# The gate weights' low parts made by ScalarE and an accumulating DMA in place of a VectorE subtraction, in a two-layer streaming encoder

## The chip, the core and the metric

The kernel runs on one core of a Trainium2 chip. Its engines are TensorE (PE, whose weight loads the profile lists as PEld), VectorE (DVE), ScalarE (ACT), GpSimd (POOL) and SyncE (SP), which here does nothing but start DMAs; the core has 16 DMA engines. The metric is the device time of one execution in microseconds (us), lower is better. Three runs of the kernel before took 2331.43, 2334.34 and 2335.2 us; their median is 2334.34 us. The profile comes from one more execution, which took 2331.33 us, with a span of 2329.6 us from the first to the last instruction.

## What is computed

Two layers of an encoder work on 1056 tokens of width 1024 (1024 prompt tokens and 32 sample tokens). Each layer is a mixer, a SwiGLU feed-forward block, and at its end a gated embedding. All of it is in float32. Cut to what this change is about:

```python
def trunk(x, ple, ...):
    for i in range(2):
        ...                                   # mixer: pooling and convolution, or gating MLP and Mamba-2
        x = layer_norm(ALPHA * x + mix, ...)
        x = layer_norm(ALPHA * x + swiglu(x, w_ff1[i], w_ff3[i], w_ff2[i]), ...)
        x = x + (ple[i] @ w_ple[i]) * sigmoid(x @ w_ple_gate[i])
```

The change concerns `w_ple_gate`, 1024 x 1024 values per layer.

## The kernel before

**Products in three parts.** TensorE reads its operands in a rounded 32-bit form (F32R). To come near full float32 accuracy the kernel writes each operand as a high part (the rounded value) and a low part (the value less its high part), and makes each product from three matmuls: high weight by high input, low weight by high input, high weight by low input.

**The weights' supply.** The class `Weights` makes the weights in the order in which they are used. For a unit of 128 x 1024 values, `raw` (L76) starts a 512 KB load on SP's queue into one of two buffers `raw`. `split` (L86) then makes both parts in a tile `w` from a ring of four: ACT copies `raw` into the high part (L88), and DVE subtracts the high part from `raw` (L89). A buffer `raw` is free for the next load but one when both have read it. `get` (L136) hands out a unit and calls `prefetch`, which emits the making of further units until two whole units (four halves) are ready beyond the one in use. The instructions of each engine stand in one order, which a scheduler fixes when the program is built; each engine takes them strictly in that order, and a DMA's wait for its buffer is made by the engine that issues it.

**The gate stage.** `embed` (L1292) first makes the eight embedding products (L1310), which ACT copies to SBUF (L1315). Then come the gate products (L1331): for each half of the tokens, t = 0 and 1, for each of eight blocks m of 128 output features, 48 matmuls of 264 columns. So each of the eight gate units is made twice a layer: 16 units a layer, 32 in all. Behind each product ACT takes the sigmoid (L1337), DVE multiplies it with the embedding (L1338) and adds it to the residual stream (L1340), and behind every second one SP stores two rows of the stream (L1343). The PSUM tiles of these products, named `q`, are four in number.

**What lies around it.** The layer norm of the first token half, made by `norm` (L1402), is finished while the embedding products run, that of the second half during the gate products of the first half. Its small chain goes PE (statistics, L1412), DVE (L1425 to L1429), POOL (L1430, L1431, L1441) and back to PE (L1456). Then come the pieces: DVE multiplies and subtracts (L1479, L1480), ACT scales (L1482), and ACT and DVE split the result into `xhgate` and `xlgate` (L323, L324), which the gate products of that half read. In layer 0 the result of each half is split once more for layer 1, by the same two lines.

Of the kernel before, what the change touches and what calls it, by code (L numbers as in the profile page):

```python
# [9 lines left out]
AF = mybir.ActivationFunctionType  # L10
ALU = mybir.AluOpType
# [41 lines left out]
class Weights:  # L53
# [43 lines left out]
    def _make(self, order):  # L97
        for kind, key, src in order:
            if kind == "steps":
                yield from src()  # L100
            elif kind == "unit":
                raw = self.raw(src)
                yield key, 2, self.split(self.place()[:, :, :src.shape[1]], raw)
            elif kind == "22":
                yield key, 1, self.split(self.half(), self.raw(src[1][:, 512:1024]))
            else:

                r0, r1 = (self.raw(v) for v in src)
                a11, a12, a21, a22 = (r[:, h * 512:(h + 1) * 512] for r in (r0, r1) for h in range(2))
                own = lambda x: (key, 1, self.split(self.half(), x))  # L110
                if kind != "sums":
                    yield own(a11)
                    yield own(a12)
                s1 = self.sub(a21, a22, ALU.add)
                s2 = self.sub(s1, a11)
                if kind == "own":
                    yield own(self.sub(a12, s2))
                    continue
                yield own(s2)
                if kind == "all":  # L120
                    yield own(s1)
                yield own(self.sub(a11, a21))
                if kind == "sums":
                    yield own(s1)
                    continue
                yield own(self.sub(a12, s2))
                yield own(a22)
# [1480 lines left out]
```

## Time and profile before

| what | value |
|---|---|
| three runs, median | 2334.34 us (2331.43 to 2335.2) |
| the profiled execution | 2331.33 us |
| its span, first to last instruction | 2329.6 us |
| TensorE busy with matmuls | 2307.0 us, 99% of the span |
| VectorE busy | 1543.4 us, 66% |
| ScalarE busy | 966.1 us, 41% |
| GpSimd busy | 71.4 us, 3% |
| mean granted TensorE clock | 0.998 |
| moved by DMA | 207.37 MB, 89 GB/s over the span |

How to read it: a busy share is the part of the span in which an engine executed instructions; the shares overlap. The groups of instructions are listed by line of the kernel, engine, operation and tiles (written <- read), with their count, the busy time in all, the mean time of one in ns, and the idle time of the engine just before them with what ended it. "SPq" rows are DMA issues on SP's queue.

The gate products begin at 1009.1 us in layer 0 and end near 1107 us; in layer 1 they end the kernel, near 2323 us.

### The profile page before, as it was taken

How to read it: one execution, taken by the hardware profiler on the slowest of the kernel's cores; microseconds unless marked ns; L12 is line 12 of the kernel's file. 1: busy time of each engine (PE TensorE's matmuls, PEld its weight loads, DVE VectorE, ACT ScalarE, POOL GpSimd, SP SyncE). 2: the span in 40 equal slices, each digit the busy share in tenths (PEclk: the TensorE clock that was granted, in tenths of full speed). 3: DMA queues.
4: the chain of work that ended last, by engine and by line, in shares of the span. 5: the costliest groups of instructions: out<-in, count | busy, mean ns of one | idle time of the engine just before them, and what ended most of it. 6: DMA issues, size and time to landing. Idle time of an engine off the chain costs nothing.

```text
span 2329.6 us, 41097 instructions
## 1 busy us (share of the span) xinstructions
PE 2307.0 (99%) x17567; PEld 2273.9 (98%) x17567; DVE 1543.4 (66%) x2426; ACT 966.1 (41%) x1616; POOL 71.4 (3%) x88
## 2 busy tenths in 40 slices
PE   9999999999999999999999999999999999999998
PEld 8999999999999999999999989999999999999998
DVE  8755787544554978775556774787554454978773
ACT  5432354333333444474543562353333333434462
POOL 0000000000000000100000120100000000000100
PEclk9999999999999999999999999999999999999999
DMA  4113123222224621124212222022222225521132
GB/s 148 47 55 127 39 68 107 74 83 74 92 73 151 239 88 44 46 83 141 80 38 66 100 85 61 19 89 94 84 73 89 73 69 205 215 69 42 37 102 91
DMA packets 84378, 207.37 MB, mean 89 GB/s; under 512 B 10236, under 2 KB 19652, under 8 KB 84196
## 3 DMA queue, kind: packets, MB, share of 16 engines
q1 hardware_dynamic: 83428, 204.07, 26.5%
q8 instruction: 137, 2.24, 0.4%
q10 hardware_dynamic: 768, 0.68, 0.1%
q14 instruction: 45, 0.37, 0.1%
HBM read 171.57 MB, written 33.16 MB: 88 GB/s over the span
## 4 chain that ended last, share of the span: by engine, by line
PE 94%; DVE 3%; DMA 1%; POOL 1%; ACT 1%; issue 0%; SPq 0%; POOLq 0%; ACTq 0%
PE q L990 38%; PE q L1203 20%; PE q L1331 8%; PE mm L228 6%; PE mm L229 6%; PE mm L230 6%; PE q L1310 2%; PE mm L639 1%; PE mm L640 1%; PE mm L641 1%; DVE bf L94 1%; PE ms L775 1%; DVE w L89 1%; DMA raw<-w_out 1%; DMA raw<-w 0%
## 5 line engine op out<-in xcount | busy, mean ns | idle before, releaser
L1203 PE MATMUL q<-w 128*128 128x264 f32 x3696 | 457.0, 285 | 0.0
L1203 PEld LDWEIGHTS q<-w 128*128 128x128 f32 x3696 | 456.1, 188 | 0.0
L88 ACT ACTIVATE w<-raw 128x512 fp32r<-128x512 f32 (+2 forms) x246 | 185.7, 774 | 221.1 <-issue 76.3
L990 PE MATMUL q<-xhin,w 128*128 128x264 f32 x1664 | 270.7, 284 | 2.0 <-ACT xhin L963 0.8
L89 DVE TENSOR_TENSOR w<-raw,w 128x512 fp32r<-128x512 f32 (+2 forms) x246 | 212.8, 878 | 55.1 <-ACT w L88 54.8
L89 DVE TENSOR_TENSOR w<-bf,w 128x512 fp32r<-128x512 f32 (+1 forms) x250 | 167.0, 691 | 106.7 <-ACT w L88 105.5
L990 PEld LDWEIGHTS q<-xhin,w 128*128 128x128 f32 x1664 | 230.1, 188 | 3.0 <-ACT xhin L963 1.0
L88 ACT ACTIVATE w<-bf 128x512 fp32r<-128x512 f32 (+1 forms) x250 | 149.0, 629 | 195.9 <-PE q L990 77.9
L990 PE MATMUL q<-xhgate,w 128*128 128x264 f32 x1280 | 207.9, 284 | 0.6 <-DVE c L886 0.6
L228 PE MATMUL mm<-xhgate,w 128*128 128x384 f32 (+1 forms) x576 | 187.5, 326 | 1.1 <-ACT xhgate L323 1.1
L230 PE MATMUL mm<-xlgate,w 128*128 128x384 f32 (+1 forms) x576 | 186.1, 324 | 0.0
L229 PE MATMUL mm<-xhgate,w 128*128 128x384 f32 (+1 forms) x576 | 185.9, 323 | 0.0
L990 PEld LDWEIGHTS q<-xhgate,w 128*128 128x128 f32 x1280 | 176.8, 188 | 1.0 <-issue 0.8
L990 PE MATMUL q<-xlin,w 128*128 128x264 f32 x832 | 169.9, 285 | 0.6 <-DVE xlin L964 0.6
L1331 PE MATMUL q<-xhgate,w 128*128 128x264 f32 x1024 | 166.7, 285 | 0.0
L1331 PEld LDWEIGHTS q<-xhgate,w 128*128 128x128 f32 x1024 | 141.6, 188 | 0.0
L990 PE MATMUL q<-xlgate,w 128*128 128x264 f32 x640 | 130.0, 285 | 0.4 <-DVE xlgate L964 0.4
L990 PEld LDWEIGHTS q<-xlin,w 128*128 128x128 f32 x832 | 128.8, 188 | 1.3 <-DVE xlin L964 1.0
L228 PE MATMUL mm<-xhin,w 128*128 128x384 f32 (+1 forms) x384 | 125.5, 328 | 3.0 <-ACT w L88 1.8
L229 PE MATMUL mm<-xhin,w 128*128 128x384 f32 (+1 forms) x384 | 124.2, 325 | 0.6 <-DVE w L89 0.6
L94 DVE TENSOR_TENSOR bf<-raw 128x512 f32<-128x512 f32 x50 | 34.5, 691 | 135.8 <-DMA raw<-w 129.8
L230 PE MATMUL mm<-xlin,w 128*128 128x384 f32 (+1 forms) x384 | 123.9, 325 | 0.0
(329 smaller groups left out, 4305.7 us busy)
## 6 DMA issues: line engine op xcount, KB each, us to landing
raw<-w SPq DMA_DIRECT2D x116, 512.0 KB, 3.6
hidden<-c SPq DMA_DIRECT2D x44, 528.0 KB, 3.0
raw<-w_gate SPq DMA_DIRECT2D x32, 512.0 KB, 3.6
raw<-w_in SPq DMA_DIRECT2D x16, 512.0 KB, 3.8
raw<-w_out SPq DMA_DIRECT2D x16, 512.0 KB, 3.6
xhdown<-hidden SPq DMA_DIRECT2D x12, 528.0 KB, 7.7
t2down<-hidden SPq DMA_DIRECT2D x8, 528.0 KB, 3.8
t3down<-hidden SPq DMA_DIRECT2D x8, 528.0 KB, 3.9
```

Source lines behind the costliest of these rows:

```text
L88: self.nc.scalar.activation(hi, x, AF.Copy)
L89: self.nc.vector.tensor_tensor(lo, x, hi.bitcast(F32), op=ALU.subtract)
L94: self.nc.vector.tensor_tensor(t, a, b, op=op)
L228: nc.tensor.matmul(ps, wh, xh, start=first, stop=False)
L229: nc.tensor.matmul(ps, wl, xh, start=False, stop=False)
L230: nc.tensor.matmul(ps, wh, xl, start=False, stop=last)
L639: nc.tensor.matmul(o, xh, hi[:, s], start=k == 0, stop=False)
L640: nc.tensor.matmul(o, xh, lo[:, s], start=False, stop=False)
L990: nc.tensor.matmul(ps[:, a, :TH // 2], w[q][:, ks], x[r][:, k, a * TH // 2:(a + 1) * TH // 2], start=not add and k == 0 and j == 0, stop=k ...
L1203: nc.tensor.matmul(ps[m][:, a, :TH // 2], v[q][:, ms], x[r][:, a * TH // 2:(a + 1) * TH // 2], start=j == 0 and n == 0, stop=j == NG - 1 a ...
L1310: nc.tensor.matmul(ps[:, b, :TH // 2], w[q][:, o:o + P], pe[k][r][:, t * TH + b * TH // 2:t * TH + (b + 1) * TH // 2], start=k == 0 and i ...
L1331: nc.tensor.matmul(ps[:, b, :TH // 2], w[q][:, ks], token_half((self.xh, self.xl), k, t, b)[r], start=k == 0 and i == 0, stop=k == KD - 1 ...
```

## The change

For units whose key begins with `w_gate`, the low part is no longer a subtraction on DVE. ACT writes the high part as before, and then, with a second instruction on the same input and a scale of -1, writes the negated high part into the place of the low part. POOL then starts a DMA that reads `raw` from SBUF and adds it to what stands there, so that the place holds the raw value less its high part. All other weights are split as before.

```diff
             elif kind == "unit":
                 raw = self.raw(src)
-                yield key, 2, self.split(self.place()[:, :, :src.shape[1]], raw)
+                t = self.place()[:, :, :src.shape[1]]
+                if key[0].startswith("w_gate"):
+                    nc = self.nc
+                    nc.scalar.activation(t[:, 0, :], raw, AF.Copy)
+                    nc.scalar.activation(t[:, 1, :], raw, AF.Copy, scale=-1.0)
+                    nc.gpsimd.dma_start(out=t[:, 1, :], in_=raw, accum_op=ALU.add)
+                    yield key, 2, (t[:, 0, :], t[:, 1, :])
+                    continue
+                yield key, 2, self.split(t, raw)
```

DVE loses 32 instructions, ACT gains 32, and POOL's queue gains 32 DMAs. TensorE's order does not change. Lines from the old L104 on stand 8 lines lower in the changed kernel: the high part is L106 there, the negated part L107, the accumulating DMA L108, and the sigmoid L1345 (L1337 before).

Two places show the new order. The first is ACT in the second token half of layer 0's gate products; `w` is a gate unit, `bf` the sigmoid's result, `q` the product in PSUM. Before:

```order
L1337 ACTIVATE bf_11044<-q_10995 128x528
L88 ACTIVATE w_11109<-raw_11107 128x1024
L1337 ACTIVATE bf_11102<-q_11053 128x528
L88 ACTIVATE w_11167<-raw_11165 128x1024
L1337 ACTIVATE bf_11161<-q_11112 128x528
```

The same stretch now:

```order
L1345 ACTIVATE bf_11055<-q_11006 128x528
L106 ACTIVATE w_11121<-raw_11119 128x1024
L107 ACTIVATE w_11121<-raw_11119 128x1024
L1345 ACTIVATE bf_11114<-q_11065 128x528
L106 ACTIVATE w_11180<-raw_11178 128x1024
L107 ACTIVATE w_11180<-raw_11178 128x1024
L1345 ACTIVATE bf_11174<-q_11125 128x528
```

Each sigmoid now has two instructions on a weight unit ahead of it where it had one.

The second place is POOL's queue in the same stage of layer 0. The rows named `rn`, `t1down` and `t2down` belong to the layer norm, `cst` holds its identity matrix. Before, the norm of the first token half is followed directly by that of the second:

```order
L1441 TENSOR_TENSOR t2down_7482<-cst,rn_0_10133 128x384
L1441 TENSOR_TENSOR t2down_7482<-cst,rn_0_10133 128x256
L1430 TENSOR_TENSOR rn_1_10579<-sm_1_10578,mhalf 128x5
L1431 TENSOR_TENSOR rn_1_10579<-sm_1_10578,rn_1_10579 128x5
L1441 TENSOR_TENSOR t1down_7550<-cst,rn_1_10579 128x384
```

And now:

```order
L1449 TENSOR_TENSOR t2down_7482<-cst,rn_0_10133 128x384
L1449 TENSOR_TENSOR t2down_7482<-cst,rn_0_10133 128x256
L108 DMA w_10165<-raw_10163 128x1024
L108 DMA w_10307<-raw_10305 128x1024
L108 DMA w_10459<-raw_10457 128x1024
L108 DMA w_10524<-raw_10522 128x1024
L1438 TENSOR_TENSOR rn_1_10583<-sm_1_10582,mhalf 128x5
```

Four of the DMAs stand between the two norms on POOL; the other twelve of the layer follow behind the second norm.

## Prediction

> **What bounds the kernel now.** I read the page's head first, then who waits for whom on TensorE, then the groups and the timeline of the gate stage. The first two lines of the page:
>
> ```profile
> span 2329.6 us, 41097 instructions
> PE 2307.0 (99%) x17567; PEld 2273.9 (98%) x17567; DVE 1543.4 (66%) x2426; ACT 966.1 (41%) x1616; POOL 71.4 (3%) x88
> ```
>
> TensorE is idle for 22.6 us in all. No other engine can give more than that back, whatever is taken from it. TensorE's waits (line, what was waited for: us in total, times, longest):
>
> ```profile
> PE ms L1456 <- POOL dg L1441: 2.7, 4, 1.0
> PE q L1456 <- POOL t1down L1441: 2.0, 2, 1.0
> PE mm L228 <- ACT w L88: 1.8, 1, 1.8
> ...
> PE q L1456 <- POOL t2down L1441: 1.3, 2, 0.6
> ```
>
> Most are the norm's, waiting for POOL; none is at L1331, the gate products. The groups say the same (busy us, mean ns | idle before):
>
> ```profile
> L1331 PE MATMUL q<-xhgate,w 128*128 128x264 f32 x1024 | 166.7, 285 | 0.0
> ```
>
> So the subtractions that leave DVE are off the path now. In layer 0's gate stage, 1009 to 1110 us, they and their neighbours by shape are:
>
> ```profile
> L89 DVE TENSOR_TENSOR w<-raw,w 128x1024 fp32r<-128x1024 f32 x18 | 21.9, 1219 | 0.8 <-ACT w L88 0.7
> L88 ACT ACTIVATE w<-raw 128x1024 fp32r<-128x1024 f32 x18 | 18.9, 1051 | 0.5 <-DMA raw<-w_gate 0.5
> L323 ACT ACTIVATE xhgate<-stream 128x1056 fp32r<-128x1056 f32 x13 | 14.1, 1082 | 2.5 <-PE q L1331 0.9 <-DVE pre L523 0.7 <-DVE stream L1340 0.7
> ```
>
> What matters instead is how a unit gets to TensorE in time. The second token half shows the rhythm undisturbed; ACT first, then DVE, then SP's queue:
>
> ```profile
> 1066.51 0.61 ACT L1337 ACTIVATE bf<-q 128x528 f32<-128x528 f32 x1 [2.49 <-PE q L1331]
> 1067.01 1.05 ACT L88 ACTIVATE w<-raw 128x1024 fp32r<-128x1024 f32 x1
> 1072.33 0.61 ACT L1337 ACTIVATE bf<-q 128x528 f32<-128x528 f32 x1 [4.27 <-PE q L1331]
> 1072.84 1.05 ACT L88 ACTIVATE w<-raw 128x1024 fp32r<-128x1024 f32 x1
> 1078.16 0.61 ACT L1337 ACTIVATE bf<-q 128x528 f32<-128x528 f32 x1 [4.27 <-PE q L1331]
> ...
> 1068.52 1.22 DVE L89 TENSOR_TENSOR w<-raw,w 128x1024 fp32r<-128x1024 f32 x1
> ...
> 1064.05 6.04 SPq L79 DMA_DIRECT2D raw<-w_gate  x2
> ...
> 1075.59 0.33 SPq L79 DMA_DIRECT2D raw<-w_gate  x1
> ```
>
> A sigmoid comes as soon as its product ends, so two products take 1078.16 - 1066.51 = 11.65 us. The high part begins 0.50 us behind a sigmoid. It is made for the product after next, so it and the low part have about 11.1 us. The second load of the pair goes out at about 1069.8 us (1064.05 + 6.04 - 0.33), just when the subtraction ends (1068.52 + 1.22 = 1069.74): with two buffers `raw`, what frees one starts the load of the unit after next.
>
> **The change, part by part.** *Removed:* 32 subtractions of 1.219 us on DVE, 39.0 us. DVE is not waited for at these products, so the path gets nothing. How full the engines are there, in the two token halves:
>
> ```profile
> 1009.00:1061.00 52.00, 52.00 (x428) 51.87 (x427) 41.86 (x48) 32.16 (x42) 4.53 (x6) 1.00 0.39 123
> 1061.00:1107.00 46.00, 46.00 (x381) 46.00 (x381) 24.42 (x29) 16.37 (x20) 0.00 (x0) 1.00 0.42 136
> ```
>
> (The columns are the length, then PE, PEld, DVE, ACT and POOL busy, the granted clock, the DMA engines' share, GB/s.) *Added on ACT:* 32 instructions on 1024 columns at 1.051 us, 33.6 us, about eight in each of these windows: ACT goes from 32.2 to some 40.6 of 52 us, and from 16.4 to 24.8 of 46. There is room, but behind them stand the sigmoids and, in the first half, the pieces of the second norm (L1482, L323). The sigmoid's cover is the four PSUM tiles; the pieces have to be done when the second half's products begin.
>
> *Added on POOL and the DMA engines:* 32 accumulating DMAs of 512 KB from SBUF to SBUF. No DMA from POOL and none that adds is in the trace, so their time X from the end of ACT's second instruction to landing is bounded. The nearest rows (KB, median us from issue to landing):
>
> ```profile
> raw<-w_gate SPq DMA_DIRECT2D x32, 512.0 KB, 3.6
> xhdown<-hidden SPq DMA_DIRECT2D x12, 528.0 KB, 7.7
> spill<-stream SPq DMA_DIRECT2D x8, 528.0 KB, 3.0
> ```
>
> Below, X is the 3.0 us of a plain store from SBUF. Above, it is the 7.7 us of transfers that share the DMA engines with others, plus 2.1 us if POOL takes as long to make it as for its slowest small instruction here (L1430, below): 9.8 us. In between I build it up: the 3.0 us store, plus one more reading of 512 KB, because an addition needs both operands, plus POOL's own time. The two windows move 123 GB/s with a share of 0.39 and 136 with 0.42, which is some 320 GB/s for all engines, so the reading takes 524 KB / 320 = 1.6 us; for POOL I take 1.6 us, the quicker of the two L1430 below. X = 3.0 + 1.6 + 1.6 = 6.2, with the waits between 6.3 us, an estimate from these rows.
>
> *The new wait.* A buffer `raw` is now free only when the accumulating DMA has landed. One turn of a buffer is load 3.6, high part 1.05, negated part 1.05, then X; it has to fit into two products: X up to 11.65 - 5.7 = 5.95 us costs nothing in the second half. Before, the same turn had 1.22 and the short wait of 0.46 us (1068.52 - 1068.06) in place of 1.05 + X. In the first half ACT is fuller, and on average I let one foreign ACT instruction of 1.08 us (L323) stand between landing and high part, which lowers the limit to 4.85. Of the 16 units of a layer two are made ahead; the other 14 are seven turns of the two buffers, four in the first half and three in the second. At X = 6.3 the turns are late by 4 x (6.3 + 1.1 - 5.95) + 3 x (6.3 - 5.95) = 5.8 + 1.05 = 6.85 us a layer. The first lateness is swallowed by the 11.1 - 2.1 - 6.3 = 2.7 us by which a unit is early. That leaves 4.15 us a layer, 8.3 us in all, all of it TensorE waiting at L1331 for its weights. At X = 3.0 it is nothing; at 9.8 it is 2 x (19.8 + 11.55 + 0.8) = 64 us (there a unit is late even with its buffer free, by 9.8 + 2.1 - 11.1).
>
> *The queues.* ACT: behind a late high part waits the sigmoid, and TensorE has three more PSUM tiles, 17 us. SP: behind a late load wait the stores of the stream, which nobody waits for. POOL: behind the fourth accumulating DMA of a layer wait the second norm's statistics; that DMA waits for its load, which waits for the second DMA. ACT handles the second unit at 1000.07 us in the trace (first row), so with 2.1 + 6.3 + 3.6 + 2.1 the fourth is issued by about 1015, and the norm's rows on POOL come later:
>
> ```profile
> 1000.07 1.06 ACT L88 ACTIVATE w<-raw 128x1024 fp32r<-128x1024 f32 x1
> ...
> 983.02 2.02 POOL L1430 TENSOR_TENSOR rn<-sm,mhalf 128x5 f32<-128x5 f32 x1 [668.50 <-ACT t2down L1315]
> 985.13 0.32 POOL L1431 TENSOR_TENSOR rn<-sm,rn 128x5 f32<-128x5 f32 x1
> 985.41 1.86 POOL L1441 TENSOR_TENSOR t1down<-cst,rn 128x384 f32<-128x384 f32 x2
> 987.23 2.32 POOL L1441 TENSOR_TENSOR t2down<-cst,rn 128x384 f32<-128x384 f32 x2
> 1024.48 1.61 POOL L1430 TENSOR_TENSOR rn<-sm,mhalf 128x5 f32<-128x5 f32 x1 [34.93 <-DVE sm L1429]
> 1026.17 0.20 POOL L1431 TENSOR_TENSOR rn<-sm,rn 128x5 f32<-128x5 f32 x1
> 1026.33 1.40 POOL L1441 TENSOR_TENSOR t1down<-cst,rn 128x384 f32<-128x384 f32 x2
> 1027.69 1.40 POOL L1441 TENSOR_TENSOR t2down<-cst,rn 128x384 f32<-128x384 f32 x2
> ```
>
> The second norm starts at 1024.48, 9 us later, so this costs nothing.
>
> *The sum.* 8.3 us on the profiled execution's 2331.33 gives 2339.6. The median of the runs lies 3.0 us above that execution, so against the median it is 2334.34 + 8.3 = 2342.6 us.
>
> **The rivals.** *The accumulating DMA is quick enough, no change.* If POOL's part is small or lies beside the transfer, X is 3.0 + 1.6 = 4.6 us, under both limits, and the time stays at 2334.3. For it: 4.6 is built from two rows, and only the third term, POOL's, is a guess. Against it: these DMAs run beside loads and stores that already fill 0.39 to 0.42 of the DMA engines. The Trainium skill, "DMA: Bandwidth & Descriptors", section on the anatomy of a DMA from GpSimd, prices one at 2.0 us plus its bytes at 436 GB/s, and "Collectives: The Full Stack", section on the bandwidth ceiling, says that the addition is slow only in that it reads two sources. My estimate from both pages is 2.0 + 2 x 1.2 = 4.4 us, and by it the sum would be this rival's; the trace of before shows neither. Chance 0.27.
>
> *The waits let the clock fall.* At the norm TensorE waited in each layer, and in layer 1 it ran at half clock afterwards:
>
> ```profile
> 2196.00:2200.00 4.00, 3.12 (x26) 2.91 (x24) 3.93 (x6) 1.91 (x4) 3.10 (x3) 1.00 0.61 152
> 2200.00:2204.00 4.00, 3.13 (x13) 2.57 (x14) 3.93 (x4) 0.61 (x1) 3.40 (x4) 0.76 0.27 111
> 2204.00:2208.00 4.00, 4.00 (x20) 4.00 (x20) 4.00 (x5) 2.15 (x4) 0.00 (x0) 0.50 0.00 0
> 2208.00:2212.00 4.00, 4.00 (x32) 4.00 (x31) 2.36 (x3) 2.50 (x5) 0.00 (x0) 0.89 0.01 2
> ```
>
> The lost clock is 4 x (0.24 + 0.50 + 0.11) = 3.4 us after 1.75 us of idling. If four of some eight new waits do this, it adds 13.6 us: 2342.6 + 13.6 = 2356.2. Against it: the mean new wait is only about 1 us. "TensorE: Matmul & The Clock Gate" in the Trainium skill, Part 1, has the clock halve after an idle window of about 3.4 us; the rows agree on the half and show it after less idling. Chance 0.13.
>
> *The accumulating DMA takes over 7.5 us,* beside other transfers or because POOL is slow: from 2 x (4 x 2.65 + 3 x 1.55 - 1.5) = 27 us to the 64 above, 2362 to 2398. Chance 0.10.
>
> *Faster.* The first norm's chain on POOL takes 983.02 to 989.55, 6.5 us, beside a busy DVE, the second norm's 1024.48 to 1029.09, 4.6 us. TensorE waits for the first. One subtraction a layer leaves DVE just there. If the chain then ran like the second, 1.9 us a layer come back, 3.8 us, and with the half-clock stretch of 3.4 us 7.2 us: 2327.1. It decides if X stays under 4.85 and DVE's load is what slows POOL. Against it: other DVE work moves up into the gap. Chance 0.05.
>
> **How the numbers follow.** A measurement of this kernel can tell about 0.2%, 4.7 us, from no change. My forecast, X between some 5 and 7.5 us with the clock held, has 0.45: 0 to +27 us, of which I put 0.10 within 4.7 us. Slower: 0.35 + 0.13 + 0.10 = 0.58. Same: 0.10 + 0.27 = 0.37. Faster: 0.05. The range runs from 2331 us, the fastest run of a kernel that has not changed, to 2370 us, which takes in the clock's rival and the lower part of the long DMA; the faster case and the longest DMAs, some 0.12, are left out. The forecast's own range is 2334 to 2362 us.
>
> **What would show it.** Right: TensorE waits at L1339 (L1331 before) for the DMA into `w`, some us a layer, first late in the first token half; the DMA rows of `w` land 6 to 6.5 us after ACT's L107; SP's loads of `raw` wait for those DMAs, not for DVE. The first step to fail would be X: under 5 us with no idle time at the gate products makes the quick rival true, over 7.5 the long one. A half clock in the gate windows would show the clock's rival. The prediction is wrong in kind if TensorE's new idle time lies at L1464 (the norm's, L1456 before) or in layer 1's mixer, or if there is none and the time still moves by over 0.2%.

## The result, and the profile after

The changed kernel is slower. Four runs of each, taken together, gave 2345.6 us (2344.48 to 2348.32) against 2334.77 us (2331.43 to 2337.43): a ratio of 1.0057, 95% interval 1.0038 to 1.0075, some 11 us. Its profiled execution took 2345.43 us. The head of its page:

```profile
span 2343.6 us, 41190 instructions
...
PE 2308.5 (99%) x17567; PEld 2273.0 (97%) x17567; DVE 1506.4 (64%) x2394; ACT 992.3 (42%) x1648; POOL 98.4 (4%) x120
```

VectorE's busy time fell by 37 us and ScalarE's rose by 26. That is less than the 33.6 us of the sum, in part because neighbouring instructions on ScalarE overlap (below, L107 starts at 1091.38, before L106 ends at 1091.47). TensorE is idle for 2343.6 - 2308.5 = 35.1 us, before for 22.6. Its waits tell where (line, what was waited for: us in total, times, longest):

```profile
PE q L1339 <- DMA w<-raw: 13.7, 11, 2.1
PE ms L1464 <- POOL dg L1449: 2.7, 4, 1.0
...
PE q L1464 <- POOL t2down L1449: 1.3, 2, 0.6
PE q L1464 <- POOL t1down L1449: 1.2, 2, 0.6
```

The first row is new: the gate products (L1339, L1331 before) wait for the accumulating DMA. The norm's waits are what they were but for 0.8 us (`t1down` 2.0 before). The same row in the second token half of layer 0 (1060 to 1113 us), then of layer 1 (2280 to 2340 us):

```profile
PE q L1339 <- DMA w<-raw: 9.0, 6, 2.1
...
PE q L1339 <- DMA w<-raw: 4.5, 4, 1.5
```

So 13.5 of the 13.7 us lie in the second halves. From 1000 to 1060 us there is no such row. The first gate products of layer 0's two halves begin with these rows:

```profile
1008.39 0.65 PE L1339 MATMUL q<-xhgate,w 128*128 128x264 f32 x4
...
1060.98 0.51 PE L1339 MATMUL q<-xhgate,w 128*128 128x264 f32 x2 [0.63 <-DMA w<-raw]
```

So the first half, with the second norm's products in it, took 1060.98 - 0.63 - 1008.39 = 52.0 us. Two windows, which part some 2 us behind this border, in the columns explained in the prediction:

```profile
1008.30:1063.00 54.70, 54.07 (x441) 53.55 (x440) 29.80 (x37) 36.86 (x47) 11.43 (x14) 1.00 0.68 164
1063.00:1113.00 50.00, 41.65 (x334) 40.62 (x333) 14.90 (x19) 19.38 (x23) 5.17 (x6) 1.00 0.76 179
```

The DMA engines went from 0.39 and 0.42 busy to 0.68 and 0.76; the granted clock stayed at 1.00. The transfers became longer, the neighbours' too (KB, median us to landing; before, the load took 3.6 and the store 3.0):

```profile
raw<-w_gate SPq DMA_DIRECT2D x32, 512.0 KB, 4.2
w<-raw POOLq DMA_DIRECT2D x32, 512.0 KB, 5.2
...
spill<-stream SPq DMA_DIRECT2D x8, 528.0 KB, 5.3
```

The spread is wide: in layer 0 the accumulating DMA's shortest, median and longest time are

```profile
DMA to landing us min/median/max: 4.5/5.5/8.5
```

One late turn, read from the timeline of the second half (POOL's issues, then SP's, then ACT's):

```profile
1055.42 0.86 POOL L108 DMA_DIRECT2D w<-raw  x1 [7.31 <-ACT w L107]
...
1075.37 0.88 POOL L108 DMA_DIRECT2D w<-raw  x1 [4.99 <-ACT w L107]
1082.13 0.86 POOL L108 DMA_DIRECT2D w<-raw  x1 [5.88 <-ACT w L107]
1092.83 0.86 POOL L108 DMA_DIRECT2D w<-raw  x1 [9.84 <-ACT w L107]
...
1104.82 0.87 POOL L108 DMA_DIRECT2D w<-raw  x1 [8.74 <-ACT w L107]
...
1083.39 4.72 SPq L79 DMA_DIRECT2D raw<-w_gate  x2
...
1090.41 1.06 ACT L106 ACTIVATE w<-raw 128x1024 fp32r<-128x1024 f32 x1 [8.19 <-DMA raw<-w_gate]
1091.38 1.04 ACT L107 ACTIVATE w<-raw 128x1024 fp32r<-128x1024 f32 x1
```

The addition issued at 1075.37 lands about 8 us later. Only then, at 1083.39, does SP start the load of the unit after next; ACT has waited 8.19 us for it when it starts at 1090.41; at 1092.42 ACT is done and at 1092.83 the next addition of this buffer goes out. That is a turn of 1092.83 - 1075.37 = 17.5 us, the longest of this half. On average, eight additions from 1055.42 to 1104.82 are (1104.82 - 1055.42) / 7 = 7.06 us apart, 14.1 us for a turn of a buffer, while TensorE asks for a unit every 11.65 / 2 = 5.83 us. 7 x (7.06 - 5.83) = 8.6 us: that is the 9.0 us of the wait's row within half a microsecond. Layer 1's second half has these rows for its first and last addition, and for TensorE's wait for the first:

```profile
2281.58 0.85 POOL L108 DMA_DIRECT2D w<-raw  x1 [7.33 <-ACT w L107]
...
2325.19 0.87 POOL L108 DMA_DIRECT2D w<-raw  x1 [3.22 <-ACT w L107]
...
2286.73 0.51 PE L1339 MATMUL q<-xhgate,w 128*128 128x264 f32 x2 [1.24 <-DMA w<-raw]
```

There the additions are (2325.19 - 2281.58) / 7 = 6.23 us apart, and the same sum gives only 2.8 of the 4.5 us; another 1.2 us are the wait for the first unit, which was late already when the half began.

### The profile page after: what moved, and what is told of

It reads as the page before. It is cut to its first block, busy times and chain, and to the rows that moved or that the text cites. A ratio compares the mean times of both kernels' runs of the same rounds, so it can differ in the third digit from the quotient of the medians.

```text
span 2343.6 us, 41190 instructions
## 1 busy us (share of the span) xinstructions
PE 2308.5 (99%) x17567; PEld 2273.0 (97%) x17567; DVE 1506.4 (64%) x2394; ACT 992.3 (42%) x1648; POOL 98.4 (4%) x120
## 5 line engine op out<-in xcount | busy, mean ns | idle before, releaser
L88 ACT ACTIVATE w<-raw 128x512 fp32r<-128x512 f32 (+2 forms) x214 | 152.3, 732 | 229.7 <-issue 76.3
L89 DVE TENSOR_TENSOR w<-raw,w 128x512 fp32r<-128x512 f32 (+2 forms) x214 | 174.1, 829 | 61.2 <-ACT w L88 61.0
L1339 PE MATMUL q<-xhgate,w 128*128 128x264 f32 x1024 | 169.8, 286 | 13.7 <-DMA w<-raw 13.7
L1339 PEld LDWEIGHTS q<-xhgate,w 128*128 128x128 f32 x1024 | 142.2, 188 | 16.1 <-DMA w<-raw 16.1
L998 PE MATMUL q<-t3sum,w 128*128 128x264 f32 x960 | 123.3, 284 | 0.0
```

Of the source, the lines that this page charges most:

```text
L88: self.nc.scalar.activation(hi, x, AF.Copy)
L89: self.nc.vector.tensor_tensor(lo, x, hi.bitcast(F32), op=ALU.subtract)
L998: nc.tensor.matmul(ps[:, a, :TH // 2], w[q][:, ks], x[r][:, k, a * TH // 2:(a + 1) * TH // 2], start=not add and k == 0 and j == 0, stop=k ...
L1339: nc.tensor.matmul(ps[:, b, :TH // 2], w[q][:, ks], token_half((self.xh, self.xl), k, t, b)[r], start=k == 0 and i == 0, stop=k == KD - 1 ...
```

## The experiments

All times are medians in us, compared with the kernel before on the same chip. The last column is TensorE's idle time ahead of the gate products, in the profiled execution.

| experiment | this | before | ratio, 95% interval | idle |
|---|---|---|---|---|
| the change itself | 2345.6 | 2334.77 | 1.0057 (1.0038 to 1.0075) | 13.7 |
| 1 third raw buffer | 2329.93 | 2332.29 | 0.9985 (0.9976 to 0.9994) | 0.0 |
| 2 addend from HBM | 2330.63 | 2332.29 | 0.9994 (0.9985 to 1.0003) | 0.0 |
| 3 addition on VectorE | 2331.0 | 2332.29 | 0.9996 (0.9987 to 1.0005) | 0.0 |
| 4 copy, no addition | 2331.24 | 2332.29 | 0.9996 (0.9987 to 1.0005) | 0.0 |
| 5 first half only | 2332.3 | 2331.32 | 1.0005 (0.9996 to 1.0014) | 1.0 |
| 6 second half only | 2332.48 | 2331.32 | 1.0008 (0.9999 to 1.0017) | 0.8 |
| 7 longer hold | 2360.24 | 2331.32 | 1.0128 (1.0114 to 1.0141) | 16.8 |
| 8 longer hold, third buffer | 2344.65 | 2331.32 | 1.0059 (1.0046 to 1.0071) | 9.4 |
| 9 units 0 to 11 | 2340.38 | 2331.75 | 1.0032 (1.0021 to 1.0044) | 9.1 |
| 10 units 4 to 11 | 2333.9 | 2331.75 | 1.0006 (0.9996 to 1.0015) | 0.0 |
| 11 late stores | 2347.07 | 2331.75 | 1.0060 (1.0048 to 1.0073) | 12.5 |
| 12 short stores in layer 0 | 2339.17 | 2331.83 | 1.0036 (1.0023 to 1.0050) | 10.2 |

The theory was the prediction's: what costs is that a `raw` buffer stays occupied until the addition has landed. The rivals were the sharing of the DMA engines as such, and ScalarE's second instruction as such.

**1, a third buffer.** Every third gate unit is loaded into a tile that is free by then.

```diff
-                raw = self.raw(src)
+                self.turn = getattr(self, "turn", -1) + key[0].startswith("w_gate")
+                if key[0].startswith("w_gate") and self.turn % 16 % 3 == 2:
+                    raw = self.temps.tile([P, 2, T], F32, tag="c", name=f"third{self.turn}")[:, 0, :src.shape[1]]
+                    self.nc.sync.dma_start(out=raw, in_=src)
+                else:
+                    raw = self.raw(src)
```

> The changed kernel with a third buffer for the gate weights' raw values (every third unit of the sixteen is loaded into the tile that held the embedding's input). Theory, the turn of the buffers: a raw buffer is held for load 4.2 + ACT 2.1 + accumulating DMA 5.5 = 11.8 us and more, against 11.65 us for two products; with three buffers it has 17.5 us, so the waits at L1339's gate products (13.7 us) shrink below 2 us and the time returns to the kernel before, 2333 to 2338 us. Rival, contention: the loads, stores and additions share the DMA engines, and the units come late whatever the buffers; then the waits stay at 10 us or more and the time at 2343 to 2348 us. Rival, ACT's second instruction per unit: also 2343 to 2348 us.

Its gate products, and its transfers:

```profile
L1344 PE MATMUL q<-xhgate,w 128*128 128x264 f32 x1024 | 166.7, 285 | 0.0
...
raw<-w_gate SPq DMA_DIRECT2D x22, 512.0 KB, 3.9
w<-raw POOLq DMA_DIRECT2D x22, 512.0 KB, 7.3
```

No idle time is left, and the whole loss is gone, although the additions now take 7.3 us, longer than in the changed kernel. A transfer of 7.3 us costs nothing as long as the loads behind it are not too late for TensorE. (SP's loads wait for landings here too, 89.8 us in all in layer 0, where it was 115.8.) This is also the only version whose interval lies below 1, by 0.15%. That is less than the 0.2% set at the start, and the profile shows only 1.0 us of it (`t1down`, 1.0 in place of 2.0); where the rest comes from stays open.

**2, the addend from HBM.** The buffer is free as soon as ACT has read it twice.

```diff
-                    nc.gpsimd.dma_start(out=t[:, 1, :], in_=raw, accum_op=ALU.add)
+                    nc.gpsimd.dma_start(out=t[:, 1, :], in_=src, accum_op=ALU.add)
```

> The accumulating DMA takes its addend from the weights in HBM and not from the raw buffer, which is then free after ACT's two readings. Theory, the turn of the buffers: the turn shortens to load 4.2 + 2.1 us, and a unit has about 11.1 us for ACT's 2.1 and the addition, 5 to 7 us; waits at the gate products below 2 us, time 2333 to 2338 us. Rival, contention: the DMA engines carry as much as in the changed kernel and HBM is read twice, so the waits stay or grow, 2343 to 2355 us. Rival, ACT's second instruction: 2343 to 2348 us.

Its additions took

```profile
w<-w_gate POOLq DMA_DIRECT2D x32, 512.0 KB, 7.8
```

The same result by another way: the raw buffer is released early instead of multiplied, with no byte less on the DMA engines and with longer additions, and the idle time is gone. With experiment 1 this rules out sharing by itself as the cause.

**3, the addition on VectorE.** ACT's second instruction stays, the DMA goes.

```diff
-                    nc.gpsimd.dma_start(out=t[:, 1, :], in_=raw, accum_op=ALU.add)
+                    nc.vector.tensor_tensor(t[:, 1, :], raw, t[:, 1, :].bitcast(F32), op=ALU.add)
```

> ACT writes the negated high part as in the changed kernel, but VectorE adds the raw values (1.22 us), so no DMA is added. Theory, the turn of the buffers: the turn is load 3.6 + 2.1 + 1.2 = 7 us, far under 11.65; no waits at the gate products, 2333 to 2337 us. Rival, contention: also 2333 to 2337 us. Rival, ACT's second instruction per unit (33.6 us more on ACT, sigmoids and pieces of the norm behind it): waits stay, 2340 to 2348 us.

ScalarE's second instruction costs nothing by itself. Against the kernel before it is also the reverse test of the purpose: VectorE has all of its old work here, and the time is that of experiments 1 and 2, where it has not.

**4, a copy in place of the addition.**

```diff
-                    nc.gpsimd.dma_start(out=t[:, 1, :], in_=raw, accum_op=ALU.add)
+                    nc.gpsimd.dma_start(out=t[:, 1, :], in_=raw)
```

> The DMA from POOL copies the raw values over the negated part and does not add (this leaves the subtraction out: the low part is the raw value). One buffer less is read. If the addition's second reading is what makes the DMA long, it lands in 3 to 4 us and not 5.2, the turn is 9.5 to 10.5 us, the waits at the gate products fall below 3 us and the time is 2334 to 2338 us. If a DMA of this size from POOL takes about 5 us anyway, the waits stay above 9 us and the time is 2342 to 2347 us.

The copy's median, POOL's queue on the DMA engines (packets, MB, share of the 16 engines' span), and the first and last copy of layer 0's second half:

```profile
q0 software_dynamic: 4608, 16.78, 2.0%
...
w<-raw POOLq DMA_DIRECT2D x32, 512.0 KB, 3.9
...
1056.78 0.53 POOL L108 DMA_DIRECT2D w<-raw  x1 [7.65 <-ACT w L107]
...
1099.22 0.53 POOL L108 DMA_DIRECT2D w<-raw  x1 [7.38 <-ACT w L107]
```

In the changed kernel the same row of the queue is

```profile
q0 software_dynamic: 4608, 16.78, 3.9%
```

The same bytes in the same packets take twice the engines' time when they are added, and the transfer takes 5.2 us instead of 3.9. With 1.3 us less the copies are (1099.22 - 1056.78) / 7 = 6.06 us apart, nearly TensorE's 5.83, and no wait comes of it.

**5 and 6, one half only.** Which of the two halves makes the loss?

```diff
-                if key[0].startswith("w_gate"):
+                self.turn = getattr(self, "turn", -1) + key[0].startswith("w_gate")
+                if key[0].startswith("w_gate") and self.turn % 16 < 8:
```

(and `>= 8` for the second half.)

> Only the eight gate units of a layer's first token half are made the new way; those of the second half keep VectorE's subtraction. Theory: in the first half TensorE has other products too (54.7 us for eight gate products in the changed kernel's window, so 13.7 us for two), and a turn of a raw buffer of some 12 to 13 us fits; the first two or three products of the second half may catch a late unit. Waits at the gate products 0 to 3 us, time 2331 to 2335 us. The prediction's step, in which each first-half turn is late by 1.45 us and the lateness adds up to 4 x 1.45 - 2.7 = 3.1 us a layer: waits of 6 us, time 2337 to 2340 us.

> Only the eight gate units of a layer's second token half are made the new way. Theory: there two products take 11.65 us and the turns were measured at about 14 us, so most of the changed kernel's 13.7 us of waiting stays; each layer gains at most the 2.7 us by which a unit is early. Waits of 8 to 13.7 us at the gate products, time 2338 to 2345 us. The prediction's step (0.35 us late a turn in this half, three turns, and 2.7 us of slack): no waits, 2331 to 2335 us.

Experiment 5 met its theory; in experiment 6 both expectations failed in part. The theory of a second half that is late by itself expected 8 us or more and got 0.8; the prediction's step expected nothing and gets the time right, but for a wrong reason. The additions of that half, first and last of eight, in experiment 6:

```profile
1047.13 1.08 POOL L109 DMA_DIRECT2D w<-raw  x1 [18.48 <-ACT w L108]
...
1096.29 0.89 POOL L109 DMA_DIRECT2D w<-raw  x1 [8.63 <-ACT w L108]
```

They are (1096.29 - 1047.13) / 7 = 7.02 us apart, as slow as in the changed kernel (7.06). The half falls behind by 7 x (7.02 - 5.83) = 8.3 us, and TensorE waits 0.8 us, at the last product. So the units stood ready about 8 us early when the half began. A lead of 8 us pays for one half, not for two.

**7 and 8, a longer hold.** The negated part is written twice, with two buffers and with three.

```diff
                     nc.scalar.activation(t[:, 1, :], raw, AF.Copy, scale=-1.0)
+                    nc.scalar.activation(t[:, 1, :], raw, AF.Copy, scale=-1.0)
```

> ScalarE writes the negated high part twice (the second writing changes no value), which holds each raw buffer 1.05 us longer. Theory, two buffers: each turn that is already late, four a layer in the second half, is 1 to 2 x 1.05 us later, and turns in the first half pass their limit too: the waits grow from 13.7 to between 20 and 30 us, time 2351 to 2362 us. Rival, a unit's own latency (not the buffer) is what is short: it has 3.5 us to spare beside 2.1 + 5.5 of 11.1 us, so 1.05 us more changes nothing, 2344 to 2348 us.

> The same second writing of the negated part, with the third raw buffer of the earlier experiment. Theory, the turn of the buffers: with three buffers the turn has 17.5 us, and the longer hold costs nothing: waits below 2 us, time 2327 to 2335 us. Rival, ScalarE's work itself (16.8 us more a layer on ScalarE, 45 of 54.7 us in the first half) delays sigmoids and high parts: 2338 to 2355 us.

Experiment 7 took the expected time by another sum. Its waits grew by only 3.1 us where 6 to 16 were expected; most of the rest is the clock. TensorE's busy time, its waits, and three windows with the clock that was granted:

```profile
PE 2317.0 (98%) x17567; PEld 2281.7 (97%) x17567; DVE 1506.7 (64%) x2394; ACT 1026.3 (44%) x1680; POOL 98.2 (4%) x120
...
PE q L1340 <- DMA w<-raw: 16.8, 12, 2.8
...
1046.00:1050.00 4.00, 3.18 (x15) 3.18 (x16) 4.00 (x6) 4.00 (x6) 0.00 (x0) 0.57 0.54 146
1054.00:1058.00 4.00, 1.24 (x6) 1.04 (x5) 0.88 (x2) 4.00 (x6) 0.87 (x1) 0.82 0.32 60
1058.00:1062.00 4.00, 4.00 (x27) 4.00 (x27) 2.38 (x3) 1.57 (x2) 0.00 (x0) 0.76 1.04 217
```

The first window lost 4 x 0.43 = 1.7 us of clock, the next two together 4 x (0.18 + 0.24) = 1.7. Three more such losses stand behind the waits near 1111, 2285 and 2325 us (and one at layer 1's norm, near 2210 us). TensorE's busy time rose by 2317.0 - 2308.5 = 8.5 us, about what the five behind gate products cost.

Experiment 8 refutes what was expected of it: the third buffer doesn't pay for the longer hold. Its two large waits in layer 0 have other causes. POOL's rows at the first, ACT's at the second:

```profile
1024.62 1.19 POOL L1444 TENSOR_TENSOR rn<-sm,mhalf 128x5 f32<-128x5 f32 x1 [4.88 <-DVE sm L1443]
...
1027.66 1.39 POOL L1455 TENSOR_TENSOR t2down<-cst,rn 128x384 f32<-128x384 f32 x2
1029.00 1.83 POOL L114 DMA_DIRECT2D w<-raw  x2
...
1050.60 1.05 ACT L111 ACTIVATE w<-raw 128x1024 fp32r<-128x1024 f32 x1
...
1052.98 1.05 ACT L112 ACTIVATE w<-raw 128x1024 fp32r<-128x1024 f32 x1
...
1055.40 1.05 ACT L113 ACTIVATE w<-raw 128x1024 fp32r<-128x1024 f32 x1
```

The additions stand behind the second norm's chain on POOL and are issued at 1029.00, together; and one unit's three instructions on ACT take from 1050.60 to 1056.45, because pieces of the norm and a sigmoid stand between them. Layer 1 has its two large waits at the same places. ScalarE's added work does matter, then, once there is twice as much of it. Experiment 8 can't say whether three buffers would have been enough.

**9 and 10, which units.** Is it the number of units in a row, or the border between the halves?

```diff
+                self.turn = getattr(self, "turn", -1) + key[0].startswith("w_gate")
-                if key[0].startswith("w_gate"):
+                if key[0].startswith("w_gate") and self.turn % 16 < 12:
```

(and `self.turn % 16 // 4 in (1, 2)` for units 4 to 11.)

> Units 0 to 11 of a layer's sixteen are made the new way, units 12 to 15 by VectorE's subtraction. Theory of the used-up lead: the first units are ready some 9 us early, each unit of the new way comes about 1.2 us later than TensorE asks for it, and TensorE waits only from the unit at which the lead is gone (unit 8 or 9); so the waits that the changed kernel had for units 8 to 11 stay, 0.6 + 2.0 + 0.3 + 1.9 in layer 0 and 1.2 + 1.5 in layer 1, some 7.5 us, and the rest go: 5 to 9 us above the kernel before. Rival, the border of the halves (the second norm's pieces on ScalarE stand between a unit's instructions there): all of the 13.7 us stay, 10 to 14 us above the kernel before.

> Units 4 to 11 are made the new way, the four before and the four behind by VectorE. Theory of the used-up lead: eight units use up what the first four kept, as in either half by itself: waits at the gate products 0 to 1.5 us, within 2 us of the kernel before. Rival, the border of the halves: the border lies in the middle of these eight, so it costs what it cost in the changed kernel, waits of 5 us or more, 4 to 12 us above the kernel before.

Eight units across the border cost nothing that can be told, twelve cost 0.32%, sixteen 0.57%. The border is refuted, the used-up lead stands: the first eight units are free wherever they lie. The 9.1 us of experiment 9 were 3.0 in layer 0 and 6.2 in layer 1, against 4.8 and 2.7 expected, so only the sum was met, and that roughly (7.5 us expected).

**11 and 12, the stores.** How much of the long turn comes from the stores that share the DMA engines?

```diff
-                    nc.sync.dma_start(out=dst[:, ms, tok], in_=self.stream[:, ms, tok])
+                    late.append((dst[:, ms, tok], self.stream[:, ms, tok]))
...
+        for out, src in late if layer == 0 else ():
+            nc.sync.dma_start(out=out, in_=src)
```

> The changed kernel, but layer 0's eight stores of the stream go out together after its last gate product; layer 1 is as it was. If the stores that share the DMA engines lengthen loads and additions, the median load in layer 0's gate stage falls from about 4.2 to 3.7 us and the addition from 5.5 to about 5 us, a turn shortens by 0.5 to 1 us, and the waits in layer 0 fall from 9 to between 4 and 6 us: the time is 2 to 5 us below the changed kernel, 6 to 9 us above the kernel before. If sharing plays no part, the waits in layer 0 stay at 8 to 9 us and the time at 10 to 13 us above the kernel before.

Experiment 11 didn't do what it was meant to. The scheduler put the stores back where they had been (L1361 is the moved line; in the changed kernel two of them stand at 1075.81 and 1088.17):

```profile
1077.36 0.43 SPq L1361 DMA_DIRECT2D spill<-stream  x1
...
1089.70 0.42 SPq L1361 DMA_DIRECT2D spill<-stream  x1
```

It is a second measurement of the change, 1.0060 after 1.0057, and says nothing of the stores. In its profiled execution the waits were 5.4 us in layer 0 and 7.0 in layer 1, where the first had 9.0 and 4.7: their sum repeats better than their place. Experiment 12 makes them short instead:

```diff
+                    if layer == 0:
+                        tok = slice(t * TH, t * TH + TH // 8)
                     nc.sync.dma_start(out=dst[:, ms, tok], in_=self.stream[:, ms, tok])
```

```diff
-                nc.sync.dma_start(out=self.acc[c], in_=self.spill[:, :, t0:t0 + n])
+                nc.sync.dma_start(out=self.acc[c], in_=self.a["xT"][:, :, t0:t0 + n])
```

> The changed kernel, but in layer 0's gate stage the eight stores of the stream write an eighth of their columns, 66 KB in place of 528 KB, and layer 1 takes its stream from the kernel's input (this leaves layer 0's sum out of the last result). Layer 1's gate stage keeps its full stores. If the stores that share the DMA engines lengthen the turn, layer 0's additions fall from 5.5 to about 5 us and its loads from 4.2 to about 3.7, a turn shortens by 0.5 to 1 us, and layer 0's waits fall from 9.0 to between 3 and 6 us, while layer 1's stay at 4 to 7: the time is 3 to 6 us below the changed kernel, 5 to 9 us above the kernel before. If the stores play no part, layer 0's waits stay at 8 to 9 us and the time at 10 to 14 us above the kernel before.

The waits and the transfers in layer 0 (965 to 1120 us), and the waits in layer 1:

```profile
PE q L1339 <- DMA w<-raw: 2.8, 3, 1.5
...
raw<-w_gate SPq DMA_DIRECT2D x16, 512.0 KB, 3.8
w<-raw POOLq DMA_DIRECT2D x16, 512.0 KB, 5.0
...
PE q L1339 <- DMA w<-raw: 7.4, 5, 3.5
```

Layer 1, with full stores, waits 7.4 us. The loss is 0.36% in place of 0.57 to 0.60. So sharing is not the cause by itself, but it seems to lengthen the turn: with 0.4 us off the load and 0.3 to 0.5 off the addition, layer 0 waited 2.8 us where the two executions of the change had 5.4 and 9.0. This rests on one profiled execution; the interval of the time (1.0023 to 1.0050) still touches that of experiment 11 (1.0048 to 1.0073).

## Why the prediction was right, and where it was not

The forecast, 2342.6 us and slower by 8.3, came within 3 us, and its mechanism held: TensorE waits at the gate products for the accumulating DMA into `w`, because a `raw` buffer is free only when that DMA has landed. Experiments 1 and 2 undo this hold in two ways, and the loss goes with it. Step by step:

- *VectorE's relief is worth nothing.* Right: with it and without it (experiments 1, 2 against 3) the time is the same.
- *ACT's second instruction has room.* Right (experiment 3).
- *X = 6.3 us.* Somewhat too long. From issue to landing it was 5.2 us in the median, 5.5 in layer 0; the prediction counts X from the end of ACT's second instruction, 0.4 us before the issue (1092.42 to 1092.83 above), so X was about 5.6 us, and 5.9 in layer 0. POOL's own part was 0.86 us and not 1.6 (the rows of L108). The copy of experiment 4, with POOL's part in it, took 3.9 us where the prediction has 3.0 + 1.6, and the addition 1.3 more where it has 1.6. The prediction took X for one number; from issue to landing it ran from 4.5 to 8.5.
- *A load takes 3.6 us.* It became 4.2, and about 7 in the late turn shown above. In the second half of layer 0 (1055 to 1113 us) the median load took 4.9 us and the median addition 5.7. That new transfers lengthen the old ones was missing from the sum, and there it mattered more than the error in X.
- *"At X = 6.3 the turns are late by 4 x (6.3 + 1.1 - 5.95) + 3 x (6.3 - 5.95)".* This step failed in its parts. It has the first half late by 1.45 us a turn and the second by 0.35. In fact the second half's turn took 14.1 us in layer 0 and 12.5 in layer 1 against 11.65, late by 2.4 and 0.8. In the first half TensorE has the second norm's products too: the half took 52.0 us, 13.0 for two products, so the limit there was not 11.65 less an ACT instruction. (The 54.7 and 13.7 us in experiment 5's expectation come from the window that reaches into the second half.)
- *A unit is early by 2.7 us.* It was about 8 (experiment 6). A ring of four tiles `w` means that a unit's high part can be written when the product four before it has ended, three products of 5.83 us ahead of its own, not two. (Counted through in the trace of before, the high part begun at 1067.01 in the prediction's rows is that of the layer's thirteenth unit, whose product begins at about 1084.0.) That leaves 17.5 - 0.5 = 17.0 us, and 17.0 - 2.1 - 6.3 = 8.6 us by the prediction's other numbers.
- *First late in the first half.* Wrong: 13.5 of 13.7 us lie in the second. The lead is used up over some eight units, and TensorE pays from then on.

The lateness was put too low in the second half and the lead too low by about 6 us a layer, and these two errors worked against each other. That the number came so near is therefore partly luck: with X as measured, 5.6 us, and its other numbers kept, the prediction's sum has turns late by 4 x (5.6 + 1.1 - 5.95) = 3.0 us and a unit early by 11.1 - 2.1 - 5.6 = 3.4 us, so no wait at all; with layer 0's 5.9 us it has 1.1 us a layer. The sum that fits layer 0 is the one under the profile, 7 x (7.06 - 5.83) = 8.6 us from the point where the lead is gone; layer 1 it fits only in part.

*The rivals.* The quick DMA was the nearest: its 4.6 us is near the shortest addition seen (4.5 from its issue, 4.9 from ACT's end). The estimate of 4.4 us from the two pages of the Trainium skill, "DMA: Bandwidth & Descriptors" and "Collectives: The Full Stack", agrees with that shortest one and not with the median of 5.2 beside loads and stores. The second page's reason, two sources to read, agrees with the queue's time, 3.9% against 2.0% for the copy. Experiment 4 shows that a quicker DMA would have made this rival true. The clock's rival did not come in the changed kernel (1.00 in both windows, no wait above 2.1 us), but it did in experiment 7, at half the price given: 1.7 us each time and not 3.4, since the stretch of before from which that price came was twice as long. The longest-DMA rival needed a median over 7.5 us; single additions were that long, the median was not. The faster case is refuted as far as it goes: the first norm's chain on POOL ran from 983.07 to 988.74 us, 0.9 us shorter than before, and gave 0.8 us in all.

```profile
983.07 1.50 POOL L1438 TENSOR_TENSOR rn<-sm,mhalf 128x5 f32<-128x5 f32 x1 [667.16 <-issue]
...
986.88 1.86 POOL L1449 TENSOR_TENSOR t2down<-cst,rn 128x384 f32<-128x384 f32 x2
```

## What to carry to other kernels

When an operation moves from an engine to a DMA, its input buffer is held until the landing: add up one whole turn of the buffer (load, every reader, landing), with the transfers as they will be beside the new ones, and compare it with the time that the consumer leaves. A turn that is too long is first paid from the lead that the ring of outputs holds, so a change that is free on eight units can cost on sixteen: compute rate and lead apart, and estimate the loss as the units behind that point times the difference of the rates (here this met layer 0 within half a microsecond, layer 1 only in part). If the turn doesn't fit, one more input buffer, or an addend read from where it still lies, cures it; here that only restores the old time, because the engine that was relieved was never waited for.

## What the runs showed of the hardware

An accumulating DMA of 512 KB within SBUF, issued by POOL, took 4.5 us at the least and 5.2 in the median beside the loads and stores of this stage, a copy of the same size 3.9; it kept POOL for 0.86 us, and its packets took twice the copy's time on the DMA engines (3.9% and 2.0% of their span).

TensorE's clock fell to half at waits of less than 3 us: in experiment 7 at waits of 2.63, 2.76, 1.91, 2.78 and 1.88 us, and each fall cost 1.7 us. The length of the wait does not decide it alone. The waits of up to 2.1 us in the changed kernel left the clock at full speed; in experiment 9 a wait of 2.83 us did so too (1.00 from 2300 to 2308 us), while one of 2.13 us did not (0.73 and 0.84 from 1074 to 1082 us). In "TensorE: Matmul & The Clock Gate", Part 1, the Trainium skill lets the clock be decided in windows of 3413 ns that run freely, whatever the kernel does. A loss of 1.7 us is half of one such window, which agrees; that a wait's place in the window decides whether it is caught would fit these waits, but no run here shows it.
